# Encoder trunk: the weight loads behind the opening are issued by GpSimd instead of SyncE

## The chip, the core and the metric

The kernel runs on one core of one Trainium2 chip. The metric is the device time of one execution in microseconds (us); lower is better. A core has five engines with a queue of instructions each: PE (TensorE, matrix products), DVE (VectorE), ACT (ScalarE), POOL (GpSimd) and SP (SyncE). SP computes nothing here; it issues DMAs. All DMAs of the core are carried out by the same 16 DMA engines.

## The reference, cut to what matters

Two requests (`x_prompt`, `x_sample`, 512 x 1024 each) go through two layers with the same weights:

```python
def encoder_layer(x, c, g_norm, w_ada, b_ada, w_in, w_out, decay_fwd, decay_bwd):
    mod = jax.nn.silu(c) @ w_ada + b_ada
    shift, scale, gate = jnp.split(mod, 3, axis=-1)
    h = rmsnorm(x, g_norm) * (1.0 + scale[:, None, :]) + shift[:, None, :]
    proj = h @ w_in
    qa, ka, va, ga, qb, kb, vb, gb = jnp.split(proj, idx, axis=-1)
    ...
    ya = oa.reshape(B, S, A_WIDTH) * jax.nn.silu(ga)
    ...
    yr = r.astype(x.dtype).reshape(B, S, R_WIDTH) * jax.nn.silu(gb)
    out = jnp.concatenate([ya, yr], axis=-1) @ w_out
    return x + gate[:, None, :] * out
```

`oa` is windowed attention with rotary position (8 heads), `r` is retention in both directions (4 heads). The weights are `w_in` (1024 x 3584 a layer), `w_out` (1024 x 1024) and the modulation weights `w_ada` (1024 x 3072).

## The kernel before, in words

Every large product is done in halves: an operand is split into a high and a low part (`wH`, `wL`; `hT`), and three products high x high, high x low, low x high are summed in PSUM. Weights come from DRAM in tiles of 128 x 1024 float32 (512 KB) named `raw` (input weights, 56 of them), `rawo` (output weights, 16) and `wa` (modulation weights, 48). ACT makes `wH` from `raw` and DVE makes `wL`; `wa` is multiplied as it is.

A query, key or retention pair goes from PE through the rotation on DVE and ACT (tiles `rc`, `rs` and others that reuse their names) to a scratch tensor in DRAM, `stk_dram` (4 stores of 256 KB), and comes back restacked as `QS`, `KS` and `KL` (6 loads of 256 KB): this is the restacking. The softmax of a pair of heads is turned by DMA transposes: `pt` becomes `pT` (64 transposes of 512 KB: 16 groups of four), and the values `vt` become `vn` (8 transposes). The group's 24 products `banks<-pT,vn` (`attn_pv`) need all four transposes. `mod_task` (called twice, 8 steps each) loads two `wa` tiles in a step and multiplies them by the condition (`banks<-wa,siluT`).

The order of the program is written by a planner at build time. The class `Plan` keeps an estimated clock for each engine (`free`) and one for the DMA engines (`dma`); `Engine` wraps each queue, issues the instruction, and tells the planner its estimated cost (`cost`, `note`). The work between the big products consists of generators that say when they could go on (`plan.at`, `plan.soon`, `plan.after`); `pump` lets them go on between the matmuls when the planner's clock of PE has come that far. So a change in a cost moves instructions on every engine. A transpose is estimated at 1250 ns on SP, then 2 bytes an element on the serial `dma` clock (262144 x 2 / 290 = 1808 ns), then 770 ns:

```python
        if eng == "SP":
            self.dma = max(end + 650.0, self.dma) + nbytes
            end = self.dma + 770.0
            eng = "DMA"
```

Instructions that use a tile made by a DMA through `plan.at` are written 1500 ns behind the estimated landing (`SLACK`).

All 494 DMAs stand in the one queue of SP, in the order in which the planner wrote them. `load_w` issues `raw` (the first five in the opening directly, the other 51 through `loader`), `load_o` issues `rawo`, `first_load` the first 16 `wa` of the opening, `mod_load` the other 32. POOL does nothing but set four constants. Every instruction is recorded through line 412 (`Engine.call`), so rows are told apart by tile names.

Of the kernel before, what the change touches and what calls it, by code (L numbers as in the profile page):

```python
# [19 lines left out]
P = 128  # L20
# [127 lines left out]
class Plan:  # L148


    def __init__(self):
        self.free = {"PE": 0.0, "DVE": 0.0, "ACT": 0.0, "SP": 0.0}
        self.dma = 3600.0
        self.ready = {}
        self.last = {}
        self.slots = {}
        self.dead = set()
        self.tasks = []
# [27 lines left out]
        t = self.soon(*tiles)  # L186
        return 0.0 if t <= self.free[eng] else t

    def note(self, eng, cost, outs, ins, nbytes=0.0):
        part = eng == "SP" and (outs[0].shape[0] < P or outs[0].tensor.name.startswith("stk"))  # L190
        outs = [k for a in outs for k in self.keys(a)]
        ins = [k for a in ins for k in self.keys(a)]
        start = self.free[eng]
        for k in ins:
            start = max(start, self.seen(eng, self.ready.get(k)))
        for k in outs:
            if not (part and self.last.get(k, (0.0, ""))[1] == "DMA"):
                start = max(start, self.seen(eng, self.last.get(k)))
        if self.dead.intersection(outs + ins):
            raise RuntimeError("use of a spare buffer")  # L200
        end = start + cost
        self.free[eng] = end
        if eng == "SP":
            self.dma = max(end + 650.0, self.dma) + nbytes
            end = self.dma + 770.0
            eng = "DMA"
        for k in outs:
            self.ready[k] = (max(end, self.ready.get(k, (0.0, ""))[0]), eng)
        for k in outs + ins:
            if end >= self.last.get(k, (0.0, ""))[0]:  # L210
                self.last[k] = (end, eng)
# [190 lines left out]
class Engine:  # L402
# [5 lines left out]
    def __getattr__(self, op):  # L408
        fn = getattr(self.eng, op)

        def call(*args, **kw):
# [7 lines left out]
                outs = pos[:1] + outs  # L419
                ins = pos[1:] + ins  # L420
            nbytes = 0.0
            if self.name == "SP":
                nbytes = outs[0].free_size() * outs[0].shape[0] * (2.0 / 290.0 if outs[0].dtype == F16 else 4.0 / 345.0)
            self.plan.note(self.name, self.cost(op, outs, ins), outs, ins, nbytes)
            return r
        return call

    def cost(self, op, outs, ins):
# [23 lines left out]
        if self.name == "ACT":  # L452
            extra = sum(1 for a in outs[1:]) + sum(1 for a in ins if a.free_size() == 1)
            return (53.0 if psum else 93.0) + 93.0 * extra + 0.833 * n
        if op == "dma_start_transpose":
            return 1250.0 * n / 1024
        return 450.0 if any("dram" in str(a.tensor.name) for a in ins + outs) else 650.0


# [1 line left out]
def trunk_kernel(  # L461
# [6 lines left out]
    nc = tc.nc  # L468
    ctx.enter_context(tc.manual_schedule())
    plan = Plan()  # L470
    V, A, T, Q = (Engine(plan, n, e) for n, e in (("DVE", nc.vector), ("ACT", nc.scalar), ("PE", nc.tensor),
                                                  ("SP", nc.sync)))
    cp = ctx.enter_context(tc.tile_pool(name="cp", bufs=1))
    st = ctx.enter_context(tc.tile_pool(name="st", bufs=4))
    pp = ctx.enter_context(tc.tile_pool(name="pp", bufs=1, space=bass.MemoryType.PSUM))
# [107 lines left out]
    def mod_load(k, parts):  # L583
        out = []
        for l, c in parts:
            t = H.take(2, "wa")
            Q.dma_start(t, split(w_ada[l, c, k], 2))
            out.append(t)
        return out

# [245 lines left out]
    jobs = [(l,) + it for l in range(DEPTH) for it in ITEMS[l]]  # L836
    raws, wts = {}, {}

    def load_w(job):
        raws[job] = []  # L840
        for h in range(ntiles(*job[1:])):
            t = W_RAW.take(1, "raw")
            Q.dma_start(t, w_in[job[0], tile_of(*job[1:], h)])
            raws[job].append(t)

    def loader(start):
        for job in jobs[start:]:
            yield lambda: W_RAW.avail(1, ntiles(*job[1:]))
            load_w(job)
        W_RAW.sure = 0  # L850

    def prepper():
# [17 lines left out]
    def load_o(l):  # L870
        for k in KORDER:
            yield lambda: min(W_RAW.avail(1), H.avail(2, 1, K_RAWO)) if len(raws) < 4 else INF
            heap = W_RAW if W_RAW.avail(1) < INF else H
            t = heap.take(1, "rawo") if heap is W_RAW else flat(heap.take(2, "rawo"))
            Q.dma_start(t, w_out[l, k * P:(k + 1) * P, :])
            raws[("O", k)] = (t, heap)

    def quiet():
# [606 lines left out]
```

## Time and profile before

| | |
|---|---|
| median of 3 runs | 1066.94 us (1066.64 to 1071.24) |
| the profiled execution | 1068.72 us, its span from first to last instruction 1066.9 us |
| granted TensorE clock | 0.999 |
| busy: PE, DVE, ACT, POOL | 98%, 72%, 44%, 0% of the span |
| DMAs | 188.69 MB on SP's queue, mean 178 GB/s |

PE is busy nearly all the time, so a change of DMA queues can take away only what PE waits for. The waits of PE show who ended each wait, the timeline of SP shows what stood ahead of a late DMA in its queue, and the windows show how busy the DMA engines were in that stretch. A busy share of DMA above 1 comes from packets whose times overlap.

### The profile page before, as it was taken

The numbers are of one execution on the slowest core, as the hardware profiler recorded it, in microseconds if no ns is written. First come the engines' busy times: TensorE is split into PE (matmuls) and PEld (weight loads), VectorE is DVE, ScalarE is ACT, GpSimd is POOL, SyncE is SP. The second block draws the span as 40 slices with busy tenths as digits, with TensorE's granted clock in tenths as the row PEclk, the third lists the DMA queues.
The fourth block names the chain that finished last, engine by engine and source line by source line (L and its number), as shares of the span: only waits on it lengthen the run. The fifth ranks groups of instructions, "written<-read, shape, count | busy, mean of one in ns | idle before, by whom it ended". The sixth has DMA issues, their size and how long they took to land.

```text
span 1066.9 us, 14779 instructions
## 1 busy us (share of the span) xinstructions
PE 1043.9 (98%) x5476; PEld 829.9 (78%) x5476; DVE 766.8 (72%) x1578; ACT 465.3 (44%) x807; POOL 0.2 (0%) x4
## 2 busy tenths in 40 slices
PE   8999999999999998999999999999999999999997
PEld 4778687777767876778888878878888787778886
DVE  5587766699668896674457885589857897776555
ACT  6364424326432565571234552427433375753011
POOL 0000000000000000000000000000000000000000
PEclk9999999999999999999999999999999999999999
DMA  8747895259964699933221796047941669962222
GB/s 350 295 139 180 238 302 209 73 194 260 273 228 139 160 244 241 234 110 137 89 90 62 240 208 221 21 139 195 244 154 51 224 119 261 244 166 99 97 101 79
DMA packets 209143, 189.63 MB, mean 178 GB/s; under 512 B 156656, under 2 KB 156944, under 8 KB 209072
## 3 DMA queue, kind: packets, MB, share of 16 engines
q1 hardware_dynamic: 209072, 188.69, 62.4%
q8 instruction: 43, 0.70, 0.3%
q14 instruction: 28, 0.23, 0.1%
HBM read 117.34 MB, written 33.57 MB: 141 GB/s over the span
## 4 chain that ended last, share of the span: by engine, by line
PE 77%; DVE 10%; DMA 6%; ACT 2%; SPq 2%; issue 2%; ACTq 0%; DVEq 0%
PE banks L412 77%; SPq L412 2%; DMA wa<-in_w_ada_dram 2%; DVE sS L412 2%; DMA pT<-pt 2%; DVE sd L412 1%; DVE pt L412 1%; DMA KL<-stk_dram 1%; DVE wL L412 1%; DVE yr L412 1%; ACT pt L412 1%; DVE rc L412 1%; DVE rs L412 1%; DVE rsq L412 1%; ACT wH L412 1%
## 5 line engine op out<-in xcount | busy, mean ns | idle before, releaser
L412 PE MATMUL banks<-hT,wH 128*128 128x512 f32 x1536 | 478.7, 392 | 0.6 <-DVE hT L412 0.2
L412 PEld LDWEIGHTS banks<-hT,wH 128*128 128x128 f32 x1536 | 285.3, 188 | 74.4 <-issue 14.1
L412 PE MATMUL banks<-hT,wL 128*128 128x512 f32 x768 | 299.2, 390 | 1.3 <-DVE wL L412 1.3
L412 PE MATMUL banks<-wo,yT 128*128 128x512 f32 (+1 forms) x792 | 175.8, 383 | 0.0
L412 PEld LDWEIGHTS banks<-hT,wL 128*128 128x128 f32 x768 | 144.2, 188 | 32.0 <-DVE wL L412 1.8
L412 PEld LDWEIGHTS banks<-wo,yT 128*128 128x128 f32 x792 | 145.2, 188 | 28.9
L412 PE MATMUL banks<-wH,hT 128*128 128x256 f32 x512 | 97.5, 284 | 0.0
L412 PEld LDWEIGHTS banks<-wH,hT 128*128 128x128 f32 x512 | 81.8, 191 | 4.8 <-issue 3.8
L412 ACT ACTIVATE sS<-sS,sm 128x512 f32<-128x512 f32 x100 | 71.1, 712 | 32.9 <-DVE sm L412 31.9
L412 DVE SCALAR_TENSOR_TENSOR pt<-sS,sm,pt 128x512 f16<-128x512 f32 x100 | 69.9, 747 | 5.0 <-DMA stk_dram<-rs 2.6
L412 PE MATMUL banks<-wL,hT 128*128 128x256 f32 x256 | 72.4, 283 | 0.0
L412 DVE TENSOR_TENSOR wL<-raw,wH 128x1024 fp32r<-128x1024 f32 x56 | 68.1, 1219 | 5.2 <-ACT wH L412 5.1
L412 ACT ACTIVATE wH<-raw 128x1024 fp32r<-128x1024 f32 x56 | 58.5, 1053 | 24.8 <-DMA raw<-in_w_in_dram 23.3
L412 ACT ACTIVATE pt<-sS,sm 128x512 f16<-128x512 f32 x100 | 65.8, 709 | 8.0 <-DVE sm L412 7.0
L412 DVE CUSTOM_DVE_ANT_0 sS<-banks,tabs 128x512 f32<-128x512 f32 x100 | 64.6, 685 | 5.7 <-PE banks L412 5.5
L412 ACT ACTIVATE sq<-xr 128x1024 bf16<-128x1024 f32 (+2 forms) x18 | 17.3, 963 | 116.4 <-DVE xr L412 92.0
L412 DVE TENSOR_TENSOR res<-banks,gb 128x512 f32<-128x512 f32 (+1 forms) x33 | 22.1, 671 | 55.1 <-PE banks L412 55.1
L412 PE MATMUL banks<-pT,vn 128*64 128x512 f16 x384 | 46.0, 381 | 5.4 <-DMA pT<-pt 5.4
L412 PEld LDWEIGHTS banks<-wL,hT 128*128 128x128 f32 x256 | 49.0, 191 | 1.0
L412 PE MATMUL banks<-sr,rv 128*128 128x512 f32 x164 | 46.0, 394 | 0.0
L412 PEld LDWEIGHTS <-vn 128*64 128x64 f16 x384 | 21.3, 109 | 27.4 <-issue 11.8
L412 PE MATMUL banks<-QS 128*128 128x512 f32 x96 | 38.1, 396 | 0.1
(309 smaller groups left out, 1215.7 us busy)
## 6 DMA issues: line engine op xcount, KB each, us to landing
raw<-in_w_in_dram SPq DMA_DIRECT2D x56, 512.0 KB, 4.7
wa<-in_w_ada_dram SPq DMA_DIRECT2D x48, 512.0 KB, 6.8
QS<-stk_dram SPq DMA_DIRECT2D x48, 256.0 KB, 4.5
KS<-stk_dram SPq DMA_DIRECT2D x48, 256.0 KB, 5.1
KL<-stk_dram SPq DMA_DIRECT2D x45, 256.0 KB, 4.6
stk_dram<-rs SPq DMA_DIRECT2D x36, 256.0 KB, 2.9
rawo<-in_w_out_dram SPq DMA_DIRECT2D x16, 512.0 KB, 4.5
stk_dram<-rc SPq DMA_DIRECT2D x24, 256.0 KB, 5.0
```

The costliest lines, as they stand in the source:

```text
L412: r = fn(*args, **kw)
```

## The change

`mod_load`, `loader` (through `load_w(job, G)`) and `load_o` issue on `G`, the queue of POOL: 32 `wa`, 51 `raw` and 16 `rawo`, 99 of 494 DMAs (51.9 MB in 512 KB tiles). The opening's loads (`first_load`, the first five `raw`, inputs and tables), restacking, transposes and stores stay on SP. The planner gets a clock for POOL with 1000 ns an issue. It charges a transpose 1175 ns on SP instead of 1250, no time on the `dma` clock, and lets it land 2200 ns after SP is done with it (`turned`).

```diff
--- before.py
+++ after.py
@@ -149,7 +149,7 @@
 
 
     def __init__(self):
-        self.free = {"PE": 0.0, "DVE": 0.0, "ACT": 0.0, "SP": 0.0}
+        self.free = {"PE": 0.0, "DVE": 0.0, "ACT": 0.0, "SP": 0.0, "POOL": 0.0}
         self.dma = 3600.0
         self.ready = {}
         self.last = {}
@@ -186,7 +186,7 @@
         t = self.soon(*tiles)
         return 0.0 if t <= self.free[eng] else t
 
-    def note(self, eng, cost, outs, ins, nbytes=0.0):
+    def note(self, eng, cost, outs, ins, nbytes=0.0, turned=False):
         part = eng == "SP" and (outs[0].shape[0] < P or outs[0].tensor.name.startswith("stk"))
         outs = [k for a in outs for k in self.keys(a)]
         ins = [k for a in ins for k in self.keys(a)]
@@ -200,7 +200,10 @@
             raise RuntimeError("use of a spare buffer")
         end = start + cost
         self.free[eng] = end
-        if eng == "SP":
+        if eng == "SP" and turned:
+            end += 2200.0
+            eng = "DMA"
+        elif eng in ("SP", "POOL"):
             self.dma = max(end + 650.0, self.dma) + nbytes
             end = self.dma + 770.0
             eng = "DMA"
@@ -419,9 +422,9 @@
                 outs = pos[:1] + outs
                 ins = pos[1:] + ins
             nbytes = 0.0
-            if self.name == "SP":
+            if self.name in ("SP", "POOL"):
                 nbytes = outs[0].free_size() * outs[0].shape[0] * (2.0 / 290.0 if outs[0].dtype == F16 else 4.0 / 345.0)
-            self.plan.note(self.name, self.cost(op, outs, ins), outs, ins, nbytes)
+            self.plan.note(self.name, self.cost(op, outs, ins), outs, ins, nbytes, op == "dma_start_transpose")
             return r
         return call
 
@@ -452,8 +455,10 @@
         if self.name == "ACT":
             extra = sum(1 for a in outs[1:]) + sum(1 for a in ins if a.free_size() == 1)
             return (53.0 if psum else 93.0) + 93.0 * extra + 0.833 * n
+        if self.name == "POOL":
+            return 1000.0
         if op == "dma_start_transpose":
-            return 1250.0 * n / 1024
+            return 1175.0 * n / 1024
         return 450.0 if any("dram" in str(a.tensor.name) for a in ins + outs) else 650.0
 
 
@@ -468,8 +473,8 @@
     nc = tc.nc
     ctx.enter_context(tc.manual_schedule())
     plan = Plan()
-    V, A, T, Q = (Engine(plan, n, e) for n, e in (("DVE", nc.vector), ("ACT", nc.scalar), ("PE", nc.tensor),
-                                                  ("SP", nc.sync)))
+    V, A, T, Q, G = (Engine(plan, n, e) for n, e in (("DVE", nc.vector), ("ACT", nc.scalar), ("PE", nc.tensor),
+                                                     ("SP", nc.sync), ("POOL", nc.gpsimd)))
     cp = ctx.enter_context(tc.tile_pool(name="cp", bufs=1))
     st = ctx.enter_context(tc.tile_pool(name="st", bufs=4))
     pp = ctx.enter_context(tc.tile_pool(name="pp", bufs=1, space=bass.MemoryType.PSUM))
@@ -584,7 +589,7 @@
         out = []
         for l, c in parts:
             t = H.take(2, "wa")
-            Q.dma_start(t, split(w_ada[l, c, k], 2))
+            G.dma_start(t, split(w_ada[l, c, k], 2))
             out.append(t)
         return out
 
@@ -836,17 +841,17 @@
     jobs = [(l,) + it for l in range(DEPTH) for it in ITEMS[l]]
     raws, wts = {}, {}
 
-    def load_w(job):
+    def load_w(job, q=Q):
         raws[job] = []
         for h in range(ntiles(*job[1:])):
             t = W_RAW.take(1, "raw")
-            Q.dma_start(t, w_in[job[0], tile_of(*job[1:], h)])
+            q.dma_start(t, w_in[job[0], tile_of(*job[1:], h)])
             raws[job].append(t)
 
     def loader(start):
         for job in jobs[start:]:
             yield lambda: W_RAW.avail(1, ntiles(*job[1:]))
-            load_w(job)
+            load_w(job, G)
         W_RAW.sure = 0
 
     def prepper():
@@ -872,7 +877,7 @@
             yield lambda: min(W_RAW.avail(1), H.avail(2, 1, K_RAWO)) if len(raws) < 4 else INF
             heap = W_RAW if W_RAW.avail(1) < INF else H
             t = heap.take(1, "rawo") if heap is W_RAW else flat(heap.take(2, "rawo"))
-            Q.dma_start(t, w_out[l, k * P:(k + 1) * P, :])
+            G.dma_start(t, w_out[l, k * P:(k + 1) * P, :])
             raws[("O", k)] = (t, heap)
 
     def quiet():
```

Three places in the order of the program.

SP in the opening, from the last loads of the input to the first restacking. Before:

```order
L412 DMA x<-in_x_sample_dram 128x1024 x4
L412 DMA tabs<-in_c_tabs_dram 128x1920
L412 DMA diff<-in_c_diff_dram 128x896
L412 DMA raw<-in_w_in_dram 128x1024
L412 DMA stk_dram_688<-rs 128x512
L412 DMA stk_dram_688<-rc 128x512
```

and now:

```order
L415 DMA x<-in_x_sample_dram 128x1024 x4
L415 DMA tabs<-in_c_tabs_dram 128x1920
L415 DMA diff<-in_c_diff_dram 128x896
L415 DMA stk_dram_688<-rs 128x512
L415 DMA stk_dram_688<-rc 128x512
```

One `raw` is gone from behind `diff`. It is the first DMA of POOL, whose queue, up to the output weights of layer 0, is now:

```order
L1485 UNCONDITIONAL_BRANCH
L415 DMA raw<-in_w_in_dram 128x1024 x5
L415 DMA wa<-in_w_ada_dram 128x1024 x16
L415 DMA raw<-in_w_in_dram 128x1024 x7
L415 DMA wa<-in_w_ada_dram 128x1024 x8
L415 DMA raw<-in_w_in_dram 128x1024 x2
L415 DMA wa<-in_w_ada_dram 128x1024 x2
L415 DMA raw<-in_w_in_dram 128x1024
L415 DMA wa<-in_w_ada_dram 128x1024 x2
L415 DMA raw<-in_w_in_dram 128x1024 x2
L415 DMA wa<-in_w_ada_dram 128x1024 x4
L415 DMA raw<-in_w_in_dram 128x1024 x6
```

Eight `rawo`, 28 `raw` and eight `rawo` follow. The first load stands behind no wait: its buffer has not been used before. All others wait for a buffer to come free.

SP in layer 0, around the transposes of a pair and the `wa` loads behind them (stk_dram_2303 and stk_dram_2411 are the scratch tensors of two pairs). Before:

```order
L412 DMA wa<-in_w_ada_dram 128x1024 x2
L412 DMA_TRANSPOSE pT<-pt 128x16x128 x4
L412 DMA QS<-stk_dram_2411 128x512
L412 DMA QS<-stk_dram_2411 128x1x512
L412 DMA KL<-stk_dram_2411 128x1x512
L412 DMA KL<-stk_dram_2411 128x512
L412 DMA KS<-stk_dram_2411 128x1x512 x2
L412 DMA wa<-in_w_ada_dram 128x1024 x2
L412 DMA raw<-in_w_in_dram 128x1024 x2
L412 DMA wa<-in_w_ada_dram 128x1024 x6
```

and now, the same kind of place (stk_dram_2274 and stk_dram_2459 take the part of those two):

```order
L415 DMA_TRANSPOSE pT<-pt 128x16x128 x3
L415 DMA KL<-stk_dram_2274 128x512
L415 DMA KS<-stk_dram_2274 128x1x512 x2
L415 DMA QS<-stk_dram_2274 128x512
L415 DMA QS<-stk_dram_2274 128x1x512
L415 DMA KL<-stk_dram_2274 128x1x512
L415 DMA_TRANSPOSE pT<-pt 128x16x128
L415 DMA stk_dram_2459<-rs 128x512
L415 DMA stk_dram_2459<-sd 128x512
L415 DMA stk_dram_2459<-rs 128x512 x2
```

No load of weights stands between transposes and restacking any more; on SP only the order of transposes, stores and restacked loads is left.

SP at the end of layer 0, where the transposes of the last two pairs meet the output weights. Before:

```order
L412 DMA_TRANSPOSE vn<-vt 128x16x128
L412 DMA raw<-in_w_in_dram 128x1024
L412 DMA rawo<-in_w_out_dram 128x1024 x2
L412 DMA_TRANSPOSE pT<-pt 128x16x128 x3
L412 DMA rawo<-in_w_out_dram 128x1024
L412 DMA_TRANSPOSE pT<-pt 128x16x128 x3
L412 DMA rawo<-in_w_out_dram 128x1024 x2
L412 DMA_TRANSPOSE pT<-pt 128x16x128 x2
L412 DMA rawo<-in_w_out_dram 128x1024 x3
L412 DMA raw<-in_w_in_dram 128x1024 x4
L412 DMA gb<-gates_d_78 128x1024 x2
```

and now:

```order
L415 DMA_TRANSPOSE pT<-pt 128x16x128 x2
L415 DMA_TRANSPOSE vn<-vt 128x16x128
L415 DMA_TRANSPOSE pT<-pt 128x16x128 x8
L415 DMA gb<-gates_d_78 128x1024 x2
L415 DMA xr<-in_x_prompt_dram 128x1024 x2
```

The eight `rawo` and the five `raw` of this place have gone to POOL, so eight `pT` transposes follow each other.

On PE the same matrix instructions are written out, in another order. The planner writes the instructions of all engines in a single sequence; counted in that, between the last transpose of a group and the group's first product stand this many matrix instructions: in layer 0, for the eight groups in order, 136, 49, 73, 81, 50, 41, 44, 33 before and 134, 36, 78, 40, 87, 54, 41, 27 now; in layer 1, 42, 33, 33, 90, 54, 38, 31, 39 before and 36, 27, 32, 66, 54, 36, 28, 27 now. For twelve of the 16 groups there are fewer.

## Rows read from the trace of the kernel before

**Rows 1.** The page: busy us, share of the span and instructions of each engine.

```profile
PE 1043.9 (98%) x5476; PEld 829.9 (78%) x5476; DVE 766.8 (72%) x1578; ACT 465.3 (44%) x807; POOL 0.2 (0%) x4
```

**Rows 2.** Timeline of PE: plain matmuls, us start, us, what.

```profile
399.16 0.62 PE L412 MATMUL banks<-hT,wH 128*128 128x512 f32 x2
399.84 0.62 PE L412 MATMUL banks<-hT,wH 128*128 128x512 f32 x2
```

**Rows 3.** The chain of waits in order of time: start us, us, what.

```profile
576.03 253.97 PE banks L412 x1348
```

**Rows 4.** Waits of PE: line, released by: us in total, times, longest.

```profile
PE banks L412 <- DMA pT<-pt: 5.4, 5, 2.3
PE banks L412 <- DMA wa<-in_w_ada_dram: 2.7, 3, 1.6
PE banks L412 <- DMA KL<-stk_dram: 1.7, 3, 1.1
```

**Rows 5.** Timeline of PE at its longest waits (idle before and releaser in brackets).

```profile
299.67 2.21 PE L412 MATMUL banks<-wa,siluT 128*32 128x512 f32 x8 [1.62 <-DMA wa<-in_w_ada_dram]
...
410.07 2.32 PE L412 MATMUL banks<-pT,vn 128*64 128x512 f16 x19 [2.31 <-DMA pT<-pt]
...
414.00 0.51 PE L412 MATMUL banks<-KL,QS 128*128 128x512 f32 x1 [1.07 <-DMA KL<-stk_dram]
...
436.39 2.35 PE L412 MATMUL banks<-pT,vn 128*64 128x512 f16 x20 [1.84 <-DMA pT<-pt]
```

**Rows 6.** Timeline of SP (DMA issues) ahead of those waits.

```profile
275.49 13.13 SPq L412 DMA_TRANSPOSE pT<-pt  x4
...
292.75 1.15 SPq L412 DMA_DIRECT2D wa<-in_w_ada_dram  x2
...
417.09 0.85 SPq L412 DMA_DIRECT2D rawo<-in_w_out_dram  x2
418.05 11.75 SPq L412 DMA_TRANSPOSE pT<-pt  x3
...
430.52 8.58 SPq L412 DMA_TRANSPOSE pT<-pt  x3
```

**Rows 7.** Busy us (x instructions) by stretch; last columns: PEclk, DMA share, GB/s.

```profile
0.00:5.00 5.00, 3.55 (x9) 1.19 (x9) 0.76 (x2) 1.46 (x2) 0.20 (x4) 1.00 0.38 107
5.00:40.00 35.00, 31.13 (x321) 20.93 (x320) 19.16 (x62) 19.41 (x28) 0.00 (x0) 1.00 1.02 407
250.00:300.00 50.00, 47.58 (x320) 37.97 (x320) 36.75 (x65) 21.77 (x39) 0.00 (x0) 1.00 1.05 274
...
608.00:640.00 32.00, 32.00 (x154) 25.26 (x153) 28.41 (x57) 19.97 (x37) 0.00 (x0) 1.00 1.06 222
```

**Rows 8.** Transposes pT: issue time ns min/median/max, and landing.

```profile
L412 SPq DMA_TRANSPOSE pT<-pt x64: 1597/2661/6569, 84.8 to 940.8; - x64
...
DMA to landing us min/median/max: 4.2/4.6/8.3
```

**Rows 9.** The 32 loads wa of 100 to 330 us, from issue to landing.

```profile
DMA to landing us min/median/max: 4.3/6.6/7.6
```

**Rows 10.** The 56 loads raw, from issue to landing.

```profile
DMA to landing us min/median/max: 3.4/4.7/10.6
```

**Rows 11.** Timeline, transposes of layer 1 and the products that use them.

```profile
618.27 16.69 SPq L412 DMA_TRANSPOSE pT<-pt  x6
626.76 2.78 PE L412 MATMUL banks<-pT,vn 128*64 128x512 f16 x24
...
940.79 3.31 SPq L412 DMA_TRANSPOSE pT<-pt  x1
948.33 2.78 PE L412 MATMUL banks<-pT,vn 128*64 128x512 f16 x24
```

**Rows 12.** Timeline of SP: the sixth load raw.

```profile
37.14 0.33 SPq L412 DMA_DIRECT2D raw<-in_w_in_dram  x1
```

**Rows 13.** DVE, groups by form: cast from SBUF to SBUF.

```profile
L412 DVE CAST hT<-h 128x512 fp32r<-128x512 f32 x23 | 9.7, 421 | 7.3 <-ACT h L412 7.3
```

## The prediction

> **What bounds the kernel now.** The page comes first: PE is busy 98% of the span, DVE 72%, ACT 44%, and POOL does nothing [rows 1]. PE works at its own pace: three plain matmuls start in 0.68 us, 0.227 us each [rows 2]. The chain of waits says the same in another way: for 253.97 us of layer 1 it stays on PE and never leaves it [rows 3]. So the queue that issues a load matters only where PE stands still, and the list of PE's waits bounds the gain. Transposes `pT` cost it 5.4 us in five waits, `wa` 2.7 us in three, restacked `KL` 1.7 us in three [rows 4]. The longest waits, on the timeline of PE, lie in layer 0 [rows 5]. The wait for `wa` of 1.62 us and the two for `pT` (2.31 and 1.84 us) and the one for `KL` (1.07 us) make 6.84 us of the 9.8 us.
>
> The timeline of SP tells why they were late. SP spent 13.13 us on four transposes, and the `wa` that PE misses at 299.67 us was issued only behind them, at 292.75 us [rows 5, 6]. Two output-weight loads went out just ahead of three transposes that took 11.75 us [rows 6]. That is the case for the change. The case against it stands in the windows: from 250 to 300 us the DMA engines were already full, at a share of 1.05 [rows 7].
>
> **The change, part by part.** The sum is made against the profiled execution, 1068.72 us; its span is 1066.9 us, and the remaining 1.8 us around it are left as they are. That execution is 1.78 us above the median of the three runs, 1066.94 us, so the forecast is the median plus the sum.
>
> *(a) `wa` leaves SP's queue.* 0.79 us of the 2.7 us of waits belong to the opening, whose `wa` stay on SP; 1.9 us can go [rows 4]. I take all of it, since POOL has nothing that holds it for 13 us as SP's transposes do. Bounds: -1.9 and 0.
>
> *(b) No weights ahead of transposes.* A load of 512 KB takes 1.29 us at the opening's 407 GB/s [rows 7], so the two `rawo` held the transposes behind them for 2.6 us, more than the wait of 1.84 us that followed [rows 5, 6]. But the rest of the transposes' time is their own: six in a row, with no weight load between them, took 16.69 us, 2.78 us each [rows 11], with the DMA engines at 1.06 [rows 7]. I take half of the 5.4 us: -2.7. Bounds: -5.4 and 0.
>
> *(c) Restacking behind fewer DMAs.* Half of `KL`'s 1.7 us [rows 4], -0.9. Bounds: -1.7 and 0.
>
> *(d) The sixth `raw` begins at the start.* SP issued it at 37.14 us [rows 12]; as POOL's first DMA it stands behind no wait. From 5 to 40 us the DMA engines are full, at a share of 1.02 and 407 GB/s; before 5 us they are at 0.38 [rows 7]. If it runs before 5 us it costs nothing; if it shares the full stretch, the opening is 512 KB later, 1.29 us. I take half, +0.6. Bounds: 0 and +1.3.
>
> *(e) Products stand closer behind their transposes.* The planner now thinks that a transpose lands 1.175 + 2.2 = 3.4 us after SP begins it, and that DMA traffic costs it nothing. The trace has 2.66 us of issue and 4.6 us to landing, both medians [rows 8], and 2.78 us between transposes in a run. It therefore writes products earlier. Twelve groups lose 119 matrix instructions of lead in all; at 0.227 us that is 27 us, the upper bound, if all of it came out as waiting. What it meets is the spare time of before, read at two groups of layer 1. A transpose lands 4.6 - 2.66 = 1.9 us after SP is done with it [rows 8]. The last of layer 1 was done at 944.1 us, so landed at about 946.0, and its products began at 948.33 us: 2.3 us spare, of which 12 instructions take 2.7. The fourth of the run that began at 618.27 us was done at 618.27 + 2 x 2.78 = 623.8 us (two of its group went before the run), landed at 625.7, and its products began at 626.76 us: 1.0 us spare, of which 6 instructions take 1.4 [rows 11]. Each becomes a wait of 0.4 us. Seven groups lose 6 instructions or more; 7 x 0.4 = +2.8. Bounds: 0 and +27.
>
> *(f) Issue and landing from POOL.* No row shows a load issued by POOL. The nearest rows are SP's: `raw` lands 4.7 us after issue, `wa` 6.6 us, 10.6 us at worst [rows 9, 10]; the longest hold on SP is a transpose's 6.57 us [rows 8]. Even at 6.57 us each the 99 loads fill 650 of 1067 us, so POOL's queue has room, and I take 0: `raw` and `rawo` are held back by buffers, not by the queue, and are used by ACT well behind their landing. If that cover went, ACT's cast would wait, then DVE's, then the matmuls. The thin place is `wa`: were each of the 16 later steps late by the 1.0 us between the median and the longest landing [rows 9], PE would lose 16 us. A quicker landing could gain nothing that (a) does not count. Bounds: 0 and +16. SP loses 99 issues that nobody waited for in themselves; the constants of the planner cost nothing but the new order.
>
> Sum: -1.9 - 2.7 - 0.9 + 0.6 + 2.8 = -2.1 us. Against the profiled execution that is 1066.6 us; against the median **1064.8 us**, less than what a measurement of this kernel can tell from no change, which I set at 0.5%, 5.3 us.
>
> **The rivals.** *All waits go.* The 9.0 us of PE's DMA waits behind the opening vanish, since no weight load holds anything up and transposes get through sooner, so that the shorter lead of (e) suffices: 1066.94 - 9.0 + 0.6 = 1058.5 us. For it: PE runs without a gap wherever DMAs are in time [rows 3]. Against it: transposes at 2.78 us each with no load near them.
>
> *Transposes too late (slower).* The planner's transpose is too cheap. It decides once the last transpose of a group lands later than its lead: 27 instructions, 6.1 us, in three groups, against 4.6 us for a lone transpose and 2.78 us more for each one queued ahead. One queued ahead is enough. If half of the 27 us comes out as waiting: 1066.94 - 1.9 - 2.7 - 0.9 + 0.6 + 13.5 = 1074.6 us. For it: the spare times of 1.0 and 2.3 us. Against it: groups that lose most had most (81 and 90 instructions), and weight loads no longer stand among the transposes.
>
> *Another queue moves nothing.* Where the DMA engines are full, as from 250 to 300 us [rows 7], a load from another queue takes from restacking and transposes what it took before: (a), (b) and (c) are 0, and the time is 1066.94 + 0.6 + 2.8 = 1070.3 us. [...] The trace agrees where the share is above 1, but the wait at 299.67 us came from 13.13 us of standing in SP's queue [rows 6], which another queue does take away.
>
> *DVE holds up POOL's issues (slower).* If a load from POOL could not be issued while DVE runs a fast cast, the 23 casts of 0.421 us [rows 13] could delay loads by 9.7 us in all; with every one on the path, 1064.8 + 9.7 = 1074.5 us. The casts belong to the making of `hT`, where `raw` has long been loaded, so little speaks for it. [...] No run here shows it yet.
>
> **How the numbers follow.** The forecast, a few waits gone and a few new ones, 0.35; all waits go, 0.28; transposes too late, 0.20; nothing moves, 0.13; DVE holds up POOL, 0.04. Faster by over 0.5% is the second case, 0.28; slower by over 0.5% the third and fifth, 0.24; within it the rest, 0.48. The likeliest case alone reaches from 1061.6 to 1070. The range takes in the case of all waits gone, and 1 us below it, 1057.5 us; above it takes in the slower cases until two thirds of the 27 us have come out as waiting, 1066.94 - 4.9 + 18 = 1080 us. What lies beyond either end I put at less than 2 in 10.
>
> **What would show it.** Right: `raw`, `wa` and `rawo` on another queue kind; PE's waits for `wa` behind the opening gone; waits for `pT` of some tenths of a us at several groups, most in layer 1 where there were nearly none; PE's first work in the opening later by 0 to 1.3 us. Wrong: PE's waits for `pT` above 10 us in all (then transposes too late), or waits for `wa` in many of the 16 steps (then (f) is mis-sized), waits as before at the same places (nothing moves), or PE busy at its pace nearly everywhere (all waits go). DVE's time in casts should stay at 9.7 us.

## The result, and the profile after

The change makes the kernel slower: 1132.7 us median of four runs (1120.61 to 1154.64) against 1069.09 us for the kernel before beside it, a ratio of 1.0507 [1.0455, 1.0558]. The ratios, here and below, leave out runs more than 1.5% above the fastest of the same kernel (two of the change's four, the profiled one among them, and one each of e2 and o1 below); the change's other two took 1120.61 and 1125.24 us. The forecast was 1064.8 us with a range to 1080; the median lies 53 us outside it. The profiled execution took 1140.17 us, its span 1138.4. The time of this kernel varies by 3% from run to run, that of the kernel before by 0.6%. So the profile shows one draw: it tells where the time goes, and the medians and ratios tell how much.

The page, part 1 (busy us of each engine) and part 3 (queues):

```profile
PE 1067.3 (94%) x5476; PEld 841.6 (74%) x5476; DVE 766.4 (67%) x1578; ACT 465.9 (41%) x807; POOL 52.6 (5%) x103
...
q1 hardware_dynamic: 194816, 136.78, 45.8%
q0 software_dynamic: 14256, 51.91, 15.1%
```

The loads did move: 51.9 MB are on a queue of their own. The span of the profiled execution grew by 71.5 us. Of that PE's idle time is 48.1 us (1138.4 - 1067.3 = 71.1, against 1066.9 - 1043.9 = 23.0 [rows 1]) and PE's busy time 23.4 us for the same 5476 matmuls. The waits of PE (total, times, longest) tell where the idle time lies:

```profile
PE banks L415 <- DMA pT<-pt: 39.9, 9, 11.8
PE banks L415 <- DMA QS<-stk_dram: 5.6, 2, 5.0
PE banks L415 <- DVE sm L415: 3.5, 1, 3.5
PE banks L415 <- DMA KL<-stk_dram: 2.9, 1, 2.9
PE banks L415 <- DMA wa<-in_w_ada_dram: 2.8, 3, 1.6
```

Waits for `pT` went from 5.4 to 39.9 us [rows 4], 34.5 of the 48.1. The longest stands at the end of layer 0. On the timeline of PE:

```profile
503.18 1.06 PE L415 MATMUL banks<-pT,vn 128*64 128x512 f16 x4 [11.76 <-DMA pT<-pt]
507.78 4.42 PE L415 MATMUL banks<-pT,vn 128*64 128x512 f16 x19 [3.54 <-DMA pT<-pt]
```

and the `pT` transposes on SP (hold ns min/median/max; first and last start us), of the whole span and of 477 to 492 us, just ahead of that wait:

```profile
L415 SPq DMA_TRANSPOSE pT<-pt x64: 1552/3224/12082, 88.0 to 1005.8; - x64
...
L415 SPq DMA_TRANSPOSE pT<-pt x2: 11727/11904/12082, 477.0 to 488.9; - x2
```

Two transposes, one behind the other with nothing between on SP, held it for 11.7 and 12.1 us, where six in a row took 2.78 us each [rows 11]; the median went from 2.66 to 3.22 us, the longest from 6.57 to 12.08 [rows 8]. Beside them ran five `rawo` that POOL issued just before and during the first of the two; they needed 3.8 to 18.9 us to land:

```profile
L415 POOL DMA_DIRECT2D rawo<-in_w_out_dram x5: 527/527/528, 471.8 to 484.6; - x5
...
DMA to landing us min/median/max: 3.8/13.5/18.9
```

The windows over that stretch (PE, PEld, DVE, ACT, POOL busy; then PEclk, DMA share, GB/s), and a stretch of the kernel before with transposes and `rawo` in one queue:

```profile
470.00:477.00 7.00, 7.00 (x44) 4.56 (x43) 6.50 (x14) 3.95 (x8) 1.58 (x3) 1.00 0.57 135
477.00:486.00 9.00, 9.00 (x42) 7.44 (x41) 7.11 (x12) 5.75 (x10) 1.05 (x2) 1.00 1.12 113
486.00:495.00 9.00, 5.42 (x24) 3.99 (x23) 3.77 (x4) 2.18 (x3) 0.00 (x0) 1.00 1.17 159
495.00:503.00 8.00, 0.00 (x0) 0.00 (x0) 1.74 (x3) 1.54 (x2) 0.00 (x0) 0.57 1.23 121
```

```profile
418.00:430.00 12.00, 12.00 (x55) 9.94 (x54) 10.14 (x23) 7.27 (x17) 0.00 (x0) 1.00 1.09 225
```

Two things stand here. The DMA engines are "busy" at a share of 1.12 to 1.23 and move only 113 to 159 GB/s; before, transposes and `rawo` in one queue moved 225 at a share of 1.09. And while PE stands still the granted clock falls: to 0.57 on the mean of 495 to 503 us, to 0.50 from 497 us on. The 19 products behind the wait then take 4.42 us, with the clock at 0.50 until 513 us; before, 19 of the same form took 2.32 us [rows 5]. So this wait is paid again behind it. In this profile the clock stood at 0.50 for 72 us, 43 of them with PE at work. The 19 products took 1.9 times as long at 0.50, so an estimate is that about half of these 43, 21.5 us, was added: most of the 23.4 us of added busy time.

POOL's own issue is as cheap as the prediction took it to be. Part 5 (count, then busy us, mean ns) and part 6 (last number: median us to landing):

```profile
L415 POOL DMA_DIRECT2D raw<-in_w_in_dram x51 | 27.2, 533 | 752.0 <-PE banks L415 362.1
...
raw<-in_w_in_dram POOLq DMA_DIRECT2D x51, 512.0 KB, 4.8
wa<-in_w_ada_dram POOLq DMA_DIRECT2D x32, 512.0 KB, 5.6
```

### The profile page after: what moved, and what is told of

Its sections match the earlier page's. It is cut to its first block, busy times and chain, and to the rows that moved or that the text cites. A ratio compares the mean times of both kernels' runs of the same rounds, so it can differ in the third digit from the quotient of the medians.

```text
span 1138.4 us, 14929 instructions
## 1 busy us (share of the span) xinstructions
PE 1067.3 (94%) x5476; PEld 841.6 (74%) x5476; DVE 766.4 (67%) x1578; ACT 465.9 (41%) x807; POOL 52.6 (5%) x103
## 4 chain that ended last, share of the span: by engine, by line
PE 42%; DVE 7%; DMA 5%; issue 1%; SPq 0%; ACT 0%; DVEq 0%; ACTq 0%
PE banks L415 42%; DMA pT<-pt 2%; DMA QS<-stk_dram 1%; DVE th L415 1%; DVE sS L415 1%; DVE pt L415 1%; DMA stk_dram<-rc 1%; DVE hT L415 1%; DVE sd L415 1%; DVE rc L415 1%; DMA stk_dram<-th 1%; DVE wL L415 1%; DMA stk_dram<-sd 0%; DVE rsq L415 0%; SPq L415 0%
## 5 line engine op out<-in xcount | busy, mean ns | idle before, releaser
L415 PE MATMUL banks<-wo,yT 128*128 128x512 f32 (+1 forms) x744 | 165.4, 383 | 0.0
L415 PEld LDWEIGHTS banks<-wo,yT 128*128 128x128 f32 x744 | 136.2, 188 | 27.0
L415 PE MATMUL banks<-pT,vn 128*64 128x512 f16 x384 | 57.0, 442 | 39.9 <-DMA pT<-pt 39.9
L415 PEld LDWEIGHTS <-vn 128*64 128x64 f16 x384 | 25.6, 123 | 67.5 <-issue 55.5
L415 ACT ACTIVATE sq<-xr 128x1024 bf16<-128x1024 f32 (+2 forms) x18 | 17.3, 963 | 116.3 <-DVE xr L415 82.2
L415 POOL DMA_DIRECT2D raw<-in_w_in_dram x51 | 27.2, 533 | 752.0 <-PE banks L415 362.1
L415 ACT ACTIVATE sS<-sS,sm 128x512 f32<-128x512 f32 x72 | 51.2, 712 | 12.9 <-DVE sm L415 12.4
L415 DVE CUSTOM_DVE_ANT_0 sS<-banks,tabs 128x512 f32<-128x512 f32 x72 | 47.4, 685 | 6.8 <-PE banks L415 6.7
L415 DVE SCALAR_TENSOR_TENSOR pt<-sS,sm,pt 128x512 f16<-128x512 f32 x72 | 50.9, 745 | 0.6 <-ACT pt L415 0.6
L415 ACT ACTIVATE pt<-sS,sm 128x512 f16<-128x512 f32 x72 | 48.0, 710 | 4.4 <-DMA vn<-vt 3.6
```

Of the source, the lines that this page charges most:

```text
L415: r = fn(*args, **kw)
```

## Experiments

Every ratio is against the kernel before, timed on the same chip beside it (1066.8 to 1067.8 us median). The change has two parts that the planner mixes: a queue (Q) and new prices, and so a new order (O).

| kernel | order of PE, DVE, ACT | loads issued by | median us of all runs (range) | ratio, 95% interval |
|---|---|---|---|---|
| e1_plan_only | new prices, planned for SP | SP | 1097.45 (1094.61 to 1100.79) | 1.0279 [1.0249, 1.0310] |
| e2_pool_only | old prices, planned for POOL | POOL | 1090.67 (1084.98 to 1105.89) | 1.0208 [1.0147, 1.0270] |
| e3_near_sp | new prices, planned for both | POOL 41, SP 58 | 1105.96 (1104.84 to 1107.72) | 1.0359 [1.0336, 1.0382] |
| o1_before_order | that of before | POOL | 1111.40 (1104.76 to 1122.96) | 1.0403 [1.0376, 1.0430] |
| o2_after_order | that of the change | SP | 1108.58 (1103.38 to 1109.49) | 1.0378 [1.0357, 1.0400] |
| d_paced | that of before | POOL, behind landed transposes | 1079.41 (1074.85 to 1082.26) | 1.0105 [1.0067, 1.0142] |
| d_wa | that of before | POOL: wa alone | 1085.73 (1083.99 to 1090.42) | 1.0176 [1.0134, 1.0218] |
| d_w | that of before | POOL: raw and rawo | 1094.98 (1093.07 to 1100.74) | 1.0255 [1.0221, 1.0289] |
| a_paced | that of the change | POOL, behind landed transposes | 1124.78 (1122.44 to 1125.89) | 1.0529 [1.0501, 1.0556] |
| c1_true_pace | price 2700 ns | SP | 1104.79 (1103.87 to 1105.73) | 1.0353 [1.0339, 1.0367] |
| c2_true_pace_pool | price 2700 ns, planned for POOL | POOL | 1124.25 (1119.25 to 1126.42) | 1.0544 [1.0529, 1.0560] |
| p1175_alone | 1175 ns on SP, nothing else | SP | 1069.16 (1067.65 to 1070.59) | 1.0017 [1.0003, 1.0031] |
| t1_adds_nothing | one half of the new price | SP | 1077.69 (1077.12 to 1081.31) | 1.0091 [1.0067, 1.0116] |
| t2_passes_loads | the other half | SP | 1073.86 (1072.47 to 1078.98) | 1.0061 [1.0041, 1.0081] |
| p2000_alone | price 2000 ns | SP | **1059.10** (1057.46 to 1059.99) | **0.9913** [0.9891, 0.9935] |
| p2200_alone | price 2200 ns | SP | 1087.70 (1087.14 to 1089.79) | 1.0192 [1.0170, 1.0213] |

"Price" is the transpose's time on the planner's DMA clock, 1808 ns before.

**The parts as the diff has them.** e1 has the change's `Plan` and prices with `G = Q`; e2 has the loads on `G` and the old prices; e3 is the change with a choice per load:

```diff
+    def near(self):
+        return self.turn + 8000.0 > self.free["PE"]
...
-            G.dma_start(t, split(w_ada[l, c, k], 2))
+            (Q if plan.near() else G).dma_start(t, split(w_ada[l, c, k], 2))
```

e1: 

> The planner's new costs of a transpose and the new order, with all loads left on SP's queue. Theory 1 (two queues in the DMA engines): near the kernel before, 1060 to 1085 us, transposes on SP at most some 7 us, waits of PE for pT below 15 us. Theory 2 (planner): as slow as the change, 1120 us or more, with waits for pT near 40 us. Theory 3 (DVE and POOL): near the kernel before.

e2: 

> The loads on POOL's queue, with the planner's old cost of a transpose (1250 ns, and its share of the DMA clock). Theory 1: most of the loss stays, 1095 to 1140 us, with single transposes of 8 us or more on SP where loads are in flight beside them. Theory 2: gone, 1060 to 1075 us. Theory 3: the loss stays, but with POOL's loads late and transposes no longer than before (6.9 us).

e3: 

> The change with one rule added: a load that the planner writes within 8 us behind the estimated landing of a transpose goes to SP's queue, the others to POOL (58 of 99 back on SP). Theory 1: most of the loss goes, 1065 to 1095 us; what is left comes from loads on POOL still in flight when a transpose begins. Theory 2: as slow as the change, 1115 us or more, since the costs are the change's. Theory 3: the loss shrinks with the share of loads on POOL, to about 1090 to 1100 us, and no single transpose is long.

Both parts cost by themselves, 2.8% and 2.1%; neither is innocent. All three times lie outside what Theories 1 and 2 named. Keeping 58 loads that the plan has near a transpose on SP (e3) gave nothing back over e1; its order is yet another one, so it can't tell why.

**The traffic by itself.** m1_stages leaves the encoder out and runs stages of eight transposes, eight loads, or both, as

```diff
+    def stage_both_pool():
+        for i in range(N):
+            load(PL, i)
+            turn(i)
```

> This kernel leaves out the whole encoder: it runs stages of DMAs one after another, each begun only when the one before has landed, and stores zeros. Stages of 8: transposes from SP alone; loads of 512 KB from POOL alone; both together (loads POOL); both from SP, alternating; both together (loads ACT); loads from SP alone; loads from SP and POOL together; loads from POOL while DVE casts. Theory 1 (two queues with transposes in one of them slow each other in the DMA engines): transposes alone 8 x 2.8 = 22 us, loads alone 8 x 1.3 = 10 us, each plus about 3 us of latency; both from SP about 33 to 36 us; both with loads on POOL 45 us or more; two queues of plain loads about 21 to 24 us, no loss. The stage with ACT tells whether it takes POOL's queue (then 33 to 36 us) or any second queue (45 us or more). Theory 2 (only the planner's costs are wrong): transposes and loads together take 33 to 36 us from whichever queue. Theory 3 (DVE holds up POOL's issues): the loads beside casts take clearly longer than the 10 us alone, 20 us or more, and both with loads on POOL is no slower than from SP.

Transposes of four stages, in order: alone, beside eight loads of POOL, alternating with eight loads in SP's queue, and beside eight loads of ACT (hold ns min/median/max; landing us min/median/max of each in the line below it):

```profile
L175 SPq DMA_TRANSPOSE pT<-pt x8: 1431/2436/3549, 32.6 to 49.9; - x8
...
DMA to landing us min/median/max: 4.4/4.8/5.5
...
L175 SPq DMA_TRANSPOSE pT<-pt x8: 1317/2294/13088, 70.7 to 98.9; - x8
...
DMA to landing us min/median/max: 4.4/4.9/17.3
...
L175 SPq DMA_TRANSPOSE pT<-pt x8: 3371/3656/3781, 105.7 to 135.9; - x8
...
DMA to landing us min/median/max: 5.4/5.7/5.9
...
L175 SPq DMA_TRANSPOSE pT<-pt x8: 1320/3349/9267, 143.2 to 176.2; - x8
...
DMA to landing us min/median/max: 4.5/8.6/18.1
```

In one queue a load delayed the transpose behind it evenly: no landing above 5.9 us. From POOL the loads went ahead (issued from 71.2 to 74.8 us, the transposes from 70.7 to 98.9) and one transpose landed after 17.3 us, although the whole stage was no longer (32.9 us against 36.3). Loads from ACT did the same, with a landing after 18.1 us, in 37.7 us: both queues beside the transposes did it, POOL's and ACT's. The 45 us for lost throughput did not come; the times are within 2 us of Theory 2's 33 to 36. Loads beside 60 of DVE's casts were issued in 4.23 us for eight and landed at a median of 7.2 us, without casts in 4.30 us and 7.3: DVE didn't hold them up.

**Queue alone, order alone.** `G` is told to the planner as the queue it is not, so the order of PE, DVE and ACT stays (the traces agree row for row, but for 6 of PE's 5476 rows in o2):

```diff
+    G = Engine(plan, "SP", nc.gpsimd)
```

in the kernel before (o1, with the three loads on `G`), and `("POOL", nc.sync)` in the changed one (o2).

o1: 

> The order of PE, DVE and ACT is row for row that of the kernel before; the planner is told that the 99 weight loads are SP's, but POOL issues them. Theory Q (in the chip, a load that POOL issues beside a transpose crowds it out, 8 to 10 us for one transpose in m1_stages): slower by 1.5 to 3%, 1083 to 1100 us, with PE's waits for pT at 15 us or more. Theory O (what the run with the loads alone on POOL lost came from the order that the planner wrote for another queue): within 0.5% of before, 1064 to 1072 us, waits for pT at 3 to 8 us.

o2: 

> The order of PE, DVE and ACT is row for row that of the changed kernel, but SP issues the 99 weight loads again, in the places that the planner gave them. Theory Q: half of the loss goes, 1095 to 1105 us, and no single transpose holds SP above 8 us. Theory O: the loss stays, 1120 to 1135 us. If SP's transposes now hold back loads that were planned for a queue of their own, waits for wa come on top, 2 to 10 us.

The queue alone costs 44.6 us on the old order by the medians (43.0 by the ratio), more than Theory Q's numbers; the order alone costs 41.8 us on SP, between the two theories. Together, in the change, they make 54 us by the ratio and 63.6 by the median, not 86. Part of the two losses may be the same standing still; no run shows that. The first line of PE's waits in o1, and the timeline of SP at the same four transposes in o1 and, in two lines, in the kernel before:

```profile
PE banks L412 <- DMA pT<-pt: 25.7, 6, 12.4
```

```profile
129.00 34.26 SPq L412 DMA_TRANSPOSE pT<-pt  x4
```

```profile
125.80 1.78 SPq L412 DMA_TRANSPOSE pT<-pt  x1
...
129.35 10.43 SPq L412 DMA_TRANSPOSE pT<-pt  x3
```

The windows of o1 around PE's longest wait (12.4 us), and that stretch of the kernel before:

```profile
134.00:142.00 8.00, 8.00 (x42) 6.08 (x40) 7.80 (x12) 1.27 (x2) 1.06 (x2) 1.00 1.07 260
142.00:150.00 8.00, 5.23 (x30) 3.70 (x23) 5.16 (x8) 1.63 (x3) 0.00 (x0) 0.98 1.27 136
150.00:158.00 8.00, 1.01 (x3) 0.18 (x3) 0.00 (x0) 0.58 (x1) 0.00 (x0) 0.50 1.29 74
```

```profile
129.00:140.00 11.00, 11.00 (x53) 8.20 (x52) 10.12 (x16) 1.45 (x3) 0.00 (x0) 1.00 1.17 228
```

Here throughput is lost: it falls from 260 to 74 GB/s at a rising share, where the kernel before moved 228. In o2 no transpose holds SP longer than 6.5 us, and other waits take their place:

```profile
PE banks L415 <- DMA wa<-in_w_ada_dram: 13.0, 8, 5.6
PE banks L415 <- DMA pT<-pt: 11.6, 5, 4.2
PE banks L415 <- DMA QS<-stk_dram: 2.8, 1, 2.8
```

**Which loads, and is it the transposes they meet?** d_wa and d_w split o1; d_paced is o1 with one tiny POOL instruction behind each transpose:

```diff
             Q.dma_start_transpose(out=split(pT.bitcast(F16), 16), in_=t.bitcast(F16))
+            nc.gpsimd.tensor_copy(seen, pT[:, 0:1].bitcast(I32))
```

d_wa: 

> Order of before; POOL issues the 32 wa of mod_load alone, SP the raw and rawo. Theory M: wa meets transposes at 125 to 165 us and at 240 to 300 us, so a part of the 44 us remains, 1075 to 1095 us. If only the loads at the ends of the layers (rawo) do the harm: 1065 to 1069 us.

d_w: 

> Order of before; POOL issues the 51 raw and 16 rawo, SP the 32 wa (the other part of o1_before_order, 44.6 us slower; the wa alone cost 18 us). If the two parts add up: 26 us, 1090 to 1097 us. If wa has to meet raw on POOL for the long stall at 150 us: less, 1070 to 1085 us, with the loss at the ends of the layers, where rawo meets eight transposes.

d_paced: 

> As o1_before_order (order of before, POOL issues the 99 loads), but POOL reads one column of each transposed tile behind its transpose, so that loads written behind a transpose begin when it has landed. Theory M (the harm comes from loads that run beside transposes): most of the 44 us comes back, 1068 to 1085 us, and no transpose holds SP above 8 us. Theory O2 (loads of another queue are late or early for PE whatever the transposes do): 1100 us or more.

The parts add up (18.1 + 27.1 = 45.2 against 44.6 us), as d_w's first case had it. d_wa shows the mechanism almost alone; timeline of SP and of POOL, and the windows:

```profile
84.75 1.82 SPq L412 DMA_TRANSPOSE pT<-pt  x1
86.68 1.63 SPq L412 DMA_DIRECT2D raw<-in_w_in_dram  x2
88.42 31.77 SPq L412 DMA_TRANSPOSE pT<-pt  x3
```

```profile
88.89 0.66 POOL L412 DMA_DIRECT2D wa<-in_w_ada_dram  x1 [88.45 <-DVE pt L412]
90.16 0.53 POOL L412 DMA_DIRECT2D wa<-in_w_ada_dram  x1 [0.60 <-DVE pt L412]
98.13 1.05 POOL L412 DMA_DIRECT2D wa<-in_w_ada_dram  x2 [7.44 <-PE banks L412]
```

```profile
93.00:106.00 13.00, 13.00 (x59) 10.78 (x58) 5.20 (x7) 2.83 (x5) 1.05 (x2) 1.00 1.15 134
106.00:120.00 14.00, 3.62 (x16) 2.65 (x15) 0.00 (x0) 0.00 (x0) 0.00 (x0) 0.75 1.26 103
```

In the kernel before the same three transposes took 9.43 us (`88.51 9.43 SPq L412 DMA_TRANSPOSE pT<-pt  x3`). Beside four `wa` from POOL, by an estimate worth 4 x 1.29 = 5.2 us of DMA time (512 KB at 407 GB/s [rows 7]), they take 31.77 us; the last two `wa` need 21 us to land. SP's next issue stands behind them, at 120.28 us, and with it the loads of `rs`, for which DVE and then PE wait: 15.6 us in PE's list under `DVE dt`, most of the 18 us. So the stall does not show as a wait for `pT` (5.7 us in that list, 5.4 before [rows 4]).

d_paced gives 32.8 of the 44.6 us back, inside Theory M's numbers: PE's waits for `pT` fall to 3.2 us and the longest hold of a transpose to 7.4 us:

```profile
PE banks L412 <- DMA pT<-pt: 3.2, 2, 2.2
```

Loads written ahead of a transpose can still run beside it; that they are what remains is likely, not shown.

**The same on the change's order.** a_paced adds the same instruction to the changed kernel.

> The changed kernel with POOL reading one column of each transposed tile behind its transpose (as d_paced). Theory M: the queue's part goes, at least to the changed order's time with SP issuing the loads (1108 us, where 13 us of waits for wa came with SP's queue), so 1090 to 1110 us, and no transpose holds SP above 8 us. If the harm on this order is not from loads beside transposes: 1120 to 1140 us.

A miss for Theory M: 1124.78 us lies in the range named for the other case and among the change's own times (1120.61 to 1154.64), and the longest hold is 8.6 us. The waits for `pT` did fall (39.9 to 10.6 us), but PE now waits for `wa`, which POOL issues behind landed transposes:

```profile
PE banks L415 <- DMA wa<-in_w_ada_dram: 16.6, 7, 3.7
PE banks L415 <- DMA pT<-pt: 10.6, 6, 4.1
```

In o2, too, it waits for `wa`, 13.0 us. That would fit an order that needs its `wa` to overtake transposes, while loads that overtake are what harms the transposes. This is argued, not shown: that the harm comes from loads beside transposes is shown on the old order alone.

**Does traffic of few loads lose throughput?** m2_stages: eight transposes and 1 to 8 loads from POOL that begin at different times; the stage that matters most is

```diff
+        for i in range(N):
+            turn(i)
+        for i in range(N):
+            begun_by(i, i // 2)
+            load(PL, i)
```

> The encoder is left out; zeros are stored. Stages of eight transposes on SP and n loads of 512 KB on POOL: none; n = 1, 2, 4, 8 loads that begin when the second transpose has landed; seven loads, one begun by each landing; eight loads, two begun by each of the first four landings; four loads, with the transposes begun by the first load's landing. Theory C (mixed traffic of two queues costs throughput): some stage with few loads takes 8 us or more beyond 22 us plus 1.3 us a load, with single transposes of 8 us or more and the DMA engines' GB/s below 130. Theory S (loads only go ahead, nothing is lost): every stage takes 22 to 24 us plus at most 1.3 us a load, and a transpose is late by what the loads beside it take.

The transposes of that stage (hold ns min/median/max):

```profile
L175 SPq DMA_TRANSPOSE pT<-pt x8: 1317/3634/9344, 208.7 to 244.6; - x8
```

Between the theories. From the first transpose's issue to the last one's end: 19.8 us with no load, 21.6, 24.6, 26.1 and 30.8 us with 1, 2, 4 and 8 loads begun together, and 28.1 us with seven begun one by one, which is close to 1.3 us a load; but 38.1 us with eight loads begun two at a time, 7.9 us more than 19.8 + 8 x 1.3, with one hold of 9.3 us. So the seven loads that met transposes one by one lost no throughput; two loads at a time lost some. That stage still moved 214 GB/s (209 to 248 us), far from the 103 and 74 in the kernel. What more is needed for the deep loss there stays open.

**The price.** p1175 to p2200 and c1 change one number, t1 and t2 one half of `turned` each:

```diff
         if eng == "SP" and turned:
-            end += 2200.0
+            end = max(end + 650.0, self.dma) + nbytes + 770.0
```

is t1; the price is set by

```diff
+                if op == "dma_start_transpose":
+                    nbytes = 2000.0 * outs[0].free_size() / 1024
```

and in t2 the line `self.dma = max(end + 650.0, self.dma) + nbytes` stands ahead of `end += 2200.0`.

c1: 

> The kernel before, its planner's price of a transpose on the DMA clock raised from 1808 to 2700 ns (the pace of 2.5 to 2.8 us that the traces show). Theory P (a transpose priced too cheap makes PE stand at its products): the 5.4 us of waits for pT fall below 3 us, 1060 to 1066 us. If the order is already good enough: 1066 to 1070 us.

c2: 

> As c1_true_pace, but the 99 weight loads are issued by POOL (planner's clock for POOL as in the change). Theory Q: the planner's single DMA clock can't know that POOL's loads go ahead of transposes; 1080 to 1095 us, near the run with the loads alone on POOL. Theory P: with products far enough behind, the queue costs nothing; 1063 to 1072 us.

p1175: 

> The kernel before with one number changed: the planner's 1250 ns on SP for a transpose is 1175 ns. Theory T (the order of before is one that fits; any price, however little it moves, gives another order that fits less): 1.5 to 3.5% slower, 1083 to 1104 us, with waits of PE at places that have little to do with a transpose. Theory P (what costs is that transposes are thought to land too early): 0.075 us a transpose is nothing, 1065 to 1071 us.

t1: 

> Loads on SP, 1250 ns on SP for a transpose as before; in the plan a transpose still lands behind the loads ahead of it (1808 + 770 ns after the DMA clock), but adds nothing to the DMA clock for those behind it. Theory A (the plan of the change loses because traffic of transposes costs the loads and restacking behind them nothing): 1085 to 1105 us, as the planner's part alone (1097 us), with waits of PE for wa, KL or QS. Theory W (it loses because transposes are thought to land whatever is queued ahead of them): 1065 to 1075 us.

t2: 

> The other half: a transpose adds its 1808 ns to the DMA clock as before, but lands 2200 ns after SP is done with it, whatever is queued ahead. Theory W: 1085 to 1105 us, with waits for pT of 5 us and more behind loads. Theory A: 1065 to 1075 us.

p2000: 

> The kernel before with the transpose's price on the DMA clock 2000 ns instead of 1808 (2700 ns cost 3.5%). If the loss grows evenly with the price: 0.7 to 0.8% slower, 1074 to 1077 us. If any new order loses: 1.5% and more, above 1083 us. If there is room between the two prices: within 0.3% of before, or a little faster, 1062 to 1070 us.

p2200: 

> As p2000_alone, at 2200 ns. If 2000 ns is near the edge of what fits: 1065 to 1085 us. If the price that fits is broad: 1055 to 1064 us.

c1 misses both its cases: 1104.79 us, and the waits for `pT` stay at 4.9 us. c2 lies above both of its theories: with the planner's price at 2700 ns, too, moving the loads (planned for POOL) costs 19 us; waits for `pT` are 14.6 us and one transpose holds SP for 13.5 us. The 75 ns on SP cost 0.2%, so a new order is not slower as such: Theory T falls. Each half of `turned` costs under 1% (9.9 and 6.0 us; t1 lies between its theories, t2 where Theory A had it), but both together, with the 75 ns, 30.6 us in e1: it is the two halves together that cost. In e1 the plan puts four `raw` directly ahead of the last two transposes of layer 0; timeline of SP, then of PE:

```profile
473.06 3.52 SPq L415 DMA_DIRECT2D raw<-in_w_in_dram  x4
477.65 8.83 SPq L415 DMA_TRANSPOSE pT<-pt  x2
```

```profile
486.14 1.06 PE L415 MATMUL banks<-pT,vn 128*64 128x512 f16 x4 [10.06 <-DMA pT<-pt]
```

The time does not follow the price evenly: 1808 ns 1066.8 us, 2000 ns 1059.1, 2200 ns 1087.7, 2700 ns 1104.8, though 2700 is about the pace that the trace shows (2.66 us by the median [rows 8], 2.78 in a row [rows 11]). 2000 ns came out faster, and 2200 slower, than any case had named. Above 2000 PE waits above all for tiles that ACT makes: at 2200 ns `ACT sr` 7.0 us and `ACT KL` 5.6, at 2700 `ACT sr` 9.6 and `ACT wo` 6.2, against 2.0 and 6.0 us for DMAs. Why ACT is late there was not followed. At 2000 ns the list has no wait for `pT` or restacking left. The page's part 1, and the first two lines of PE's waits:

```profile
PE 1039.1 (98%) x5476; PEld 829.0 (79%) x5476; DVE 767.3 (73%) x1578; ACT 463.2 (44%) x803; POOL 0.2 (0%) x4
```

```profile
PE banks L412 <- DVE yr L412: 2.3, 1, 2.3
PE banks L412 <- DVE th L412: 1.5, 2, 0.9
```

This is the version that beats both kernels: SP's single queue, one number changed, 0.9% faster than before. Four prices can't tell a good price from one lucky order.

## Why the prediction was wrong

- **(a) `wa` leaves SP's queue, -1.9.** It held in full: from 40 us on PE has no wait for `wa` in the changed kernel, nor in o1; the 2.8 us in the list all lie in the opening. It is the only gain.
- **(b) No weights ahead of transposes, -2.7, bounds -5.4 and 0.** This is the step that failed first. It took a load out of the transposes' queue and with it out of their way; the upper bound of 0 excluded a loss, and no row gave a reason for that. With the order untouched (o1) the waits for `pT` rise from 5.4 to 25.7 us, and the queue costs 44.6 us. SP's queue had also been a pace: a load behind a transpose began behind it (before, SP's transposes of 129.35 us ended at 139.78, and the `raw` behind them went out at 139.88). From POOL it began when its buffer was free, beside the transpose (in d_wa two `wa` at 98.13 us, with the three transposes holding SP from 88.42 to 120.19); d_paced puts the pace back and 32.8 us return.
- **(c) Restacking, -0.9.** Wrong in sign: `KL` 2.9 and `QS` 5.6 us against 1.7 for `KL` before. Of restacking, the order alone (o2) makes PE wait 4.3 us and the queue alone (o1) 2.5, so it comes from both.
- **(d) The sixth `raw`, +0.6, bounds 0 and 1.3.** Too small. PE's wait for `wL` in the opening ends at 28.90 us in o1 against 27.27 before, 1.6 us later; with this `raw` on SP it ends at 27.14 us on the new order (o2). In the changed kernel it ends at 30.43 us; there the granted clock from 0 to 20 us was 0.87, where it was 1.00 before. From 0 to 50 us it was 0.93 in the changed kernel, 0.97 in o1 and 1.00 before; in o1 the slow products (32 of `wa` in 1.47 us, later in 1.08) begin at 29.69 us, behind that wait.
- **(e) Products closer behind their transposes, +2.8, bounds 0 and 27.** This step failed too: the order alone costs 41.8 us (o2), beyond the bound. It counted only the lead between a transpose and its product. It left out that the new order also moves loads: four `raw` stand ahead of the last two transposes of layer 0 in e1, and PE waits 13.0 us for `wa` in o2. And the wait is paid again in clock: in o2 PE is busy 1064.7 us against 1043.9, at a mean granted clock of 0.984 against 0.999.
- **(f) Issue and landing from POOL, 0.** Right: 0.53 us an issue, `wa` landed in 5.6 us (6.6 on SP [rows 9]), `raw` in 4.8 (4.7 [rows 10]), all medians.
- **Not in the sum at all: the clock** (a mean of 0.968), by the estimate of 21.5 us most of the 23.4 us of added busy time in the profiled execution. The kernel before had no row for it at 0.999.

Of the rivals, "transposes too late" had the sign and half of the mechanism, at about a seventh of the loss (its sum gives 1075.5 us, not 1074.6). The sign named for it, waits for `pT` above 10 us, came, but does not tell it from the queue: with the old order (o1) they are 25.7 us. "DVE holds up POOL's issues" falls with m1_stages: eight loads were issued in 4.23 us beside casts and in 4.30 us without. "Another queue moves nothing" falls in the other direction: `wa` from POOL and transposes from SP were in flight together in d_wa, and on the old order another queue cost 44.6 us (o1). The transposes were the ones to yield, with holds of up to 12 to 14 us where the longest before was 6.57, and in o1 and d_wa both together fell to 74 and 103 GB/s.

Open: what turns mixed traffic into the deep loss, why the pace gave nothing back on the change's order, and why both halves of `turned` cost twice what they cost apart.

## What to carry to other kernels

A queue is also an order: before loads are given one of their own, ask what they will then run beside, and price that from both sides. Where a planner writes the program, hold its order fixed (tell it the old queue and issue on the new) and then hold the queue fixed; here the two parts showed only so. The planner's price that made this program fastest (2000 ns) was not the measured duration (2660 ns by the median [rows 8]): scan it, in small steps.

## What the runs showed of the hardware that was not expected

- Loads from POOL and transposes from SP at the same time moved as little as 74 to 136 GB/s at a DMA share of 1.15 to 1.29 (o1, d_wa), where mixed traffic in SP's one queue moved 225 and 228 at 1.09 and 1.17; a single transpose then held SP for up to 13.9 us (o1) and 14.4 us (d_wa). With seven loads begun one by one (m2_stages) nothing was lost: 28.1 us, against 19.8 + 7 x 1.3 = 28.9. Loads from ACT crowded out a transpose as those from POOL did: it landed after 18.1 and 17.3 us, where none took more than 5.9 us in one queue (m1_stages).
- While PE stood idle, its granted clock was 0.57 (495 to 503 us of the changed kernel) and 0.50 (150 to 158 us of o1, 1.01 us of work), and the 19 products behind the first took 4.42 us instead of 2.32. In the profile of the changed kernel each us of added idle time came with another half us of PE's busy time (23.4 on 48.1).
